# Log-sum-exp on one core: in three of the last four half units, three heads biased on TensorE and folded by GpSimd

## Chip, cores and metric

One core of a Trainium2 chip. The metric is the device time of one execution in microseconds (us). All inputs and outputs are fp32. The profile's own span is about 2 us shorter than the device time, so times inside a trace are compared with times inside another trace, and totals with totals. Ratios of totals are computed as the mean time of one kernel's fast runs over the mean time of the other's fast runs of the same rounds, so they are not quite the ratio of the medians quoted beside them.

## The reference

```python
B, S, D, H = 8, 2048, 2048, 8            # Dh = D // H = 256
x_heads = x.reshape(B, S, H, Dh).transpose(0, 2, 1, 3) + bias[None, :, None, :]
x_tiled = np.repeat(x_heads, 2, axis=2)
mx = x_tiled.max(axis=-1, keepdims=True)
lse = mx.squeeze(-1) + np.log(np.exp(x_tiled - mx).sum(axis=-1))
```

For each row and each of 8 heads: add a bias of 256 numbers, exponentiate, sum, take the logarithm, write it twice. The kernel leaves out the maximum, which random normal inputs allow.

## The kernel before

There are two ways to account for the bias: add it before the exponential (TensorE adds it in PSUM, or GpSimd in SBUF), or multiply the exponential by the *factor* exp(bias) while summing (VectorE's multiply-and-reduce, called a weighted sum below; or a multiply on GpSimd). In this kernel x is loaded into SBUF, and PSUM holds what TensorE puts out and the factors of heads 1 to 6. Rows come in units of 256; late units are split into two half units of 128 rows. I call the last four half units 62a, 62b, 63a, 63b. Each stage shares the 8 heads among the engines:

```python
# pe: heads biased on TensorE; acc: of these, summed by ScalarE's accumulator;
# fold: heads at the upper end multiplied and folded by GpSimd; the rest: weighted sums on VectorE
PROMPT_F1 = dict(pe=2, acc=2, g0=8, late=False, fold=1)
PROMPT_F2 = dict(pe=2, acc=2, g0=8, late=False, fold=2)
SINGLE_F1 = dict(pe=1, acc=1, g0=8, late=False, fold=1)
TRIPLE = dict(pe=3, acc=3, g0=8, late=False, fold=0)
# BULK and MIXED, the body: cut
FOLD = 32
STAGES = [(0, (BULK,)), (54, (MIXED,)), (57, (PROMPT_F1, PROMPT_F1)),
          (62, (SINGLE_F1, SINGLE_F1)), (63, (PROMPT_F2, TRIPLE))]
```

GpSimd's fold multiplies by the factor, then adds halves in place until 32 columns a head are left, which VectorE reduces:

```python
def fold(t, k, h0, h1, sums, after):
    v = xts[t % NBUF][:, k, h0 * Dh : h1 * Dh]
    done = nc.gpsimd.tensor_tensor(out=v, in0=v, in1=w_sb[...], op=ALU.mult)
    ...
    while n > FOLD:
        n //= 2
        done = nc.gpsimd.tensor_tensor(out=v[:, :, 0:n], in0=v[:, :, 0:n], in1=v[:, :, n:2*n], op=ALU.add)
    def add_up(): ...                      # the short reduction on VectorE, recorded later
```

The order on each engine is the order of recording. For one half unit, cut to what matters here:

```python
heads = add_x(...)                         # TensorE adds x to the bias in PSUM
bias_there = put_bias(next half unit)
keep_warm()                                # three dummy matmuls, results unused: to keep the clock up
flush(for_pool)                            # the short reductions of earlier folds, and so on
done = exp_inplace(...)                    # ScalarE: exponential of the SBUF heads
flush(for_pe)                              # ScalarE: exponential of the PREVIOUS half unit's PSUM heads
weigh(...)                                 # VectorE
```

The softmax here doesn't subtract the row's maximum and nothing guards it: scores larger than these inputs give would overflow.

## Time and profile before

| | before |
|---|---|
| time, median of 3 (range) | 325.56 us (325.21 to 325.87) |
| span of the profiled run | 323.1 us |
| busy in the span | PE 84%, VectorE (DVE) 88%, ScalarE (ACT) 82%, GpSimd (POOL) 89% |
| all transfers (loads and stores) | 135.42 MB at 419 GB/s |
| end of each engine's work in the tail | DVE 319.63, ACT 319.43, POOL 319.17 |

Read the table from below: the share of busy time says little in a kernel whose body is paced by loads and whose change lies in the last 15 us. What counts is when each engine finishes its part of the last half units, and there three engines end within 0.5 us of each other. The lines behind this are in the prediction.

### The profile page before, as it was taken

What the parts mean: (1) busy time and instruction counts of PE and PEld (TensorE: products, weight loads), DVE (VectorE), ACT (ScalarE), POOL (GpSimd) and SP (SyncE); (2) the same over time, 40 slices, a digit from 0 to 9 for tenths busy, and PEclk for the clock granted to TensorE, in tenths of its full rate; (3) what the DMA queues carried; (4) which work ended last, traced back from release to release, by engine and by line L of the source; (5) the groups of instructions that cost most, each with busy time, mean ns of one, the idle gap of its engine ahead of it and who ended that gap; (6) DMA issues with size and microseconds to landing.
All of it is one profiled execution on the core that took longest, in us unless ns stands there. A gap on an engine that the chain in (4) does not pass through costs nothing.

```text
span 323.1 us, 2398 instructions
## 1 busy us (share of the span) xinstructions
PE 270.3 (84%) x691; PEld 102.9 (32%) x691; DVE 283.9 (88%) x306; ACT 265.8 (82%) x426; POOL 287.7 (89%) x120
## 2 busy tenths in 40 slices
PE   5999999889978769977869886888997786599984
PEld 2333333333323223322323322333333232035442
DVE  1037779999999998999899899898999999999995
ACT  1148679889869976988888978889998998899995
POOL 6939998999999999999999999999999999858874
PEclk9979799979979996998997997997999999559998
DMA  8999999999999999999999999999999999999995
GB/s 311 457 402 454 450 400 439 450 402 446 438 414 446 432 418 443 430 422 447 422 426 441 422 434 442 404 426 430 432 422 431 430 428 425 416 422 421 419 401 170
DMA packets 8830, 135.42 MB, mean 419 GB/s; under 512 B 1041, under 2 KB 1425, under 8 KB 2417
## 3 DMA queue, kind: packets, MB, share of 16 engines
q1 hardware_dynamic: 8720, 135.27, 98.6%
q8 instruction: 5, 0.08, 0.1%
q14 instruction: 7, 0.06, 0.0%
q10 hardware_dynamic: 98, 0.01, 0.0%
HBM read 134.23 MB, written 1.05 MB: 419 GB/s over the span
## 4 chain that ended last, share of the span: by engine, by line
DMA 40%; POOL 18%; ACT 17%; PE 14%; DVE 9%; issue 0%; SPq 0%; DVEq 0%
DMA xb<-in_x_dram 40%; POOL xb L376 18%; ACT xb L382 11%; DVE R L401 6%; PE pair L326 5%; PE one_ps L326 3%; PE pair L267 3%; ACT xb L357 2%; PE one_ps L267 2%; DVE xb L417 2%; PE pair L219 1%; ACT xb L337 1%; DVE xb L394 1%; ACT res L471 1%; ACT xb L344 1%; DMA brow<-in_bias_dram 1%
## 5 line engine op out<-in xcount | busy, mean ns | idle before, releaser
L376 POOL TENSOR_TENSOR xb<-xb,b_rep 128x2048 f32<-128x2048 f32 x57 | 257.6, 4539 | 20.7 <-DMA xb<-in_x_dram 20.6
L401 DVE TENSOR_REDUCE R<-xb 128x14 f32<-128x3584 f32 (+1 forms) x56 | 214.5, 3830 | 1.9
L382 ACT ACTIVATE xb<-xb 128x2560 f32<-128x2560 f32 (+5 forms) x77 | 157.1, 2050 | 10.3 <-POOL xb L376 10.1
L326 PE MATMUL pair<-xb,ident 128*128 128x512 f32 x216 | 114.3, 656 | 0.0
L326 PE MATMUL one_ps<-xb,ident 128*128 128x512 f32 x108 | 67.5, 710 | 11.5 <-DMA xb<-in_x_dram 11.5
L344 ACT ACTIVATE xb<-pair 128x1024 f32<-128x1024 f32 x54 | 55.5, 1027 | 23.2 <-PE pair L326 23.0
L326 PEld LDWEIGHTS pair<-xb,ident 128*128 128x128 f32 x216 | 46.2, 214 | 61.3 <-issue 61.3
L394 DVE TENSOR_TENSOR xb<-xb,w_ps 128x512 f32<-128x512 f32 x54 | 36.7, 681 | 26.2 <-ACT xb L382 26.2
L337 ACT ACTIVATE xb<-one_ps 128x256 f32<-128x256 f32 x108 | 40.0, 380 | 6.6 <-PE one_ps L326 6.6
L267 PEld LDWEIGHTS <-ones 3*128 3x128 bf16 (+1 forms) x192 | 16.9, 95 | 80.8 <-issue 71.4
L267 PE MATMUL one_ps<-b,ones 3*128 3x512 bf16 x49 | 18.6, 380 | 25.4 <-ACT xb L337 25.3
L267 PE MATMUL pair<-b,ones 3*128 3x512 bf16 x98 | 29.0, 375 | 0.0
L326 PEld LDWEIGHTS one_ps<-xb,ident 128*128 128x128 f32 x108 | 17.2, 200 | 33.9 <-DMA xb<-in_x_dram 18.0
L302 PE MATMUL pair<-xb,ident 128*128 128x512 f32 (+1 forms) x36 | 21.7, 689 | 5.7 <-DMA xb<-in_x_dram 5.7
L417 DVE CUSTOM_DVE_ANT_0 xb<-xb,w_ps 128x256 f32<-128x256 f32 x61 | 22.4, 418 | 0.0
L337 ACT ACTIVATION_READ_ACCUMULATOR xb<-one_ps 128x1 f32 x108 | 22.3, 207 | 0.0
L441 POOL TENSOR_TENSOR xb<-xb 128x128 f32<-128x128 f32 (+3 forms) x39 | 13.8, 355 | 3.1
L433 POOL TENSOR_TENSOR xb<-xb,w_sb 128x256 f32<-128x256 f32 (+1 forms) x13 | 10.0, 771 | 5.2 <-ACT xb L382 4.5
L317 PE MATMUL tp<-ident 128*128 128x128 f32 x84 | 13.7, 302 | 0.0
L317 PEld LDWEIGHTS tp<-ident 128*128 128x128 f32 x84 | 11.1, 200 | 3.5 <-issue 3.0
L357 ACT ACTIVATE xb<-pair 128x256 f32<-128x256 f32 x33 | 11.9, 364 | 0.0
L417 DVE CUSTOM_DVE_ANT_0 xb<-xb,one_ps 128x256 f32<-128x256 f32 x27 | 10.6, 415 | 0.1
(42 smaller groups left out, 83.4 us busy)
## 6 DMA issues: line engine op xcount, KB each, us to landing
xb<-in_x_dram SPq DMA_DIRECT2D x20, 4096.0 KB, 21.5
xb<-in_x_dram SPq DMA_DIRECT2D x17, 2048.0 KB, 22.7
xb<-in_x_dram SPq DMA_DIRECT2D x12, 1024.0 KB, 22.7
xb<-in_x_dram SPq DMA_DIRECT2D x4, 256.0 KB, 13.2
out_dram<-res SPq DMA_DIRECT2D x1, 896.0 KB, 6.7
xb<-in_x_dram SPq DMA_DIRECT2D x2, 384.0 KB, 15.8
xb<-in_x_dram SPq DMA_DIRECT2D x2, 128.0 KB, 6.3
out_dram<-res_last SPq DMA_DIRECT2D x1, 128.0 KB, 1.7
```

Of the source, the lines that this page charges most:

```text
L267: nc.tensor.matmul(p, lhsT=lhsT, rhs=each_row(b, h * Dh, Dh, K), start=i == 0, stop=False,)
L302: mm = nc.tensor.matmul(p, lhsT=ident, rhs=xts[t % NBUF][:, ka:kb, c : c + w], start=False, stop=True,)
L317: nc.tensor.matmul(tp[:, 0], lhsT=ident, rhs=ident, start=True, stop=True)
L326: mm = nc.tensor.matmul(p, lhsT=ident, rhs=xts[t % NBUF][:, :, h * Dh : (h + 1) * Dh], start=False, stop=True,)
L337: act = nc.scalar.activation(out=xts[t % NBUF][:, k, 0:Dh], in_=got[0][:, k * Dh : (k + 1) * Dh], func=ACT.Exp, accum_out=sums[:, k, 0:1],)
L344: act = nc.scalar.activation(out=xts[t % NBUF][:, :, Dh : m["pe"] * Dh].rearrange("p k (h j) -> p h k j", j=Dh), in_=got[-1].rearrange("p ...
L357: act = nc.scalar.activation(out=xts[t % NBUF][:, k, h * Dh : (h + 1) * Dh], in_=p, func=ACT.Exp, accum_out=sums[:, k, h : h + 1],)
L376: add = nc.gpsimd.tensor_tensor(out=v, in0=v, in1=each_row(b_rep, c - G0, D - c, k1 - k0), op=ALU.add)
L382: return on_x(t, nc.scalar.activation(out=v, in_=v, func=ACT.Exp), [after])
L394: mul = nc.vector.tensor_tensor(out=f, in0=f, in1=each_row(w_ps, m["pe"] * Dh - W0, n, k1 - k0), op=ALU.mult,)
L401: red = nc.vector.tensor_reduce(out=sums[:, k0:k1, h0:H], in_=v.rearrange("p k (h j) -> p k h j", j=Dh), op=ALU.add, axis=mybir.AxisListTy ...
L417: ttr = nc.vector.tensor_tensor_reduce(out=v, in0=v, in1=w, scale=1.0, scalar=0.0, op0=ALU.mult, op1=ALU.add, accum_out=dst,)
```

## The change

The intent: in 62a, 62b and 63a TensorE biases three heads in place of one or two. One activation exponentiates all three out of two PSUM banks, without accumulator reads, and GpSimd folds them, without a multiply as the bias is in already. VectorE keeps heads 3 to 7. TensorE, with more real work, drops its dummy matmuls in all four. The core of the diff:

```diff
-PROMPT_F2 = dict(pe=2, acc=2, g0=8, late=False, fold=2)
-SINGLE_F1 = dict(pe=1, acc=1, g0=8, late=False, fold=1)
+FOLDED = dict(pe=3, acc=0, g0=8, late=False, fold=0)
-    (62, (SINGLE_F1, SINGLE_F1)),
-    (63, (PROMPT_F2, TRIPLE)),
+    (62, (FOLDED, FOLDED)),
+    (63, (FOLDED, TRIPLE)),
-    [(0, 512), (1280, 2048), (512, 1280)],
+    [(0, 768), (1280, 2048), (768, 1280)],
...
+    def exp_biased(t, k, n, heads):
+        _, _, bank, _, mm = heads[-1]
+        act = nc.scalar.activation(out=xts[t % NBUF][:, k, 0 : n * Dh],
+                                   in_=pairs[bank // 2][:, 0 : n * Dh], func=ACT.Exp)
...
+                    if m["acc"] == 0:
+                        done = exp_biased(t, k, m["pe"], heads)
+                        for_pool.append(fold(t, k, 0, m["pe"], sums, done))
+                        return
...
-                if next_units and not m["late"]:
-                    bias_there = put_bias(*next_units.pop(0))
-                if t > T_PROMPT and m["g0"] == H:
+                if t > T_PROMPT and m["g0"] == H and m["pe"] * Dh <= MM:
                     keep_warm()
...
-            if c0 == 0:
+            if c0 == 0 or t == T - 1 and k0 == 0:
                 flush(for_pe)
+            if c0 == 0 and next_units and not m["late"]:
+                bias_there = put_bias(*next_units.pop(0))
```

The rest of the diff lets the fold skip its multiply, lets a reader of two banks be ordered against both, and aligns a three-head half unit to a pair of banks.

More of the change, by code (lines that the diff above doesn't have):

```diff
@@ L244, with on_bank @@
     bank_users = [[], []]
-    def on_bank(i, ins):
-        for j, u in bank_users[i // 2]:
-            if j != i and u.ins.engine != ins.ins.engine:
+    def on_bank(i, ins, both=False):
+        pair = i // 2
+        i = None if both else i
+        for j, u in bank_users[pair]:
+            if None not in (i, j) and j != i and u.ins.engine != ins.ins.engine:
                 tc.declare_no_dep(ins.ins, u.ins, reason="another bank")
-        bank_users[i // 2].append((i, ins))
+        bank_users[pair].append((i, ins))
         return ins
@@ L275, in put_bias @@
         n = m["pe"] * Dh
+        if n > MM:
+            n_ps[0] += n_ps[0] % 2
         rows = min(k1 - k0, max(MM // n, 1))
@@ L313, in add_x @@
         return heads
+    def exp_biased(t, k, n, heads):
+        _, _, bank, _, mm = heads[-1]
+        act = nc.scalar.activation(
+            out=xts[t % NBUF][:, k, 0 : n * Dh],
+            in_=pairs[bank // 2][:, 0 : n * Dh],
+            func=ACT.Exp,
+        )
+        on_bank(bank, on_x(t, act, [mm]), both=True)
+        return act
     def keep_warm():
@@ L432, in fold @@
         v = xts[t % NBUF][:, k, h0 * Dh : h1 * Dh]
-        done = nc.gpsimd.tensor_tensor(
-            out=v, in0=v, in1=w_sb[:, h0 * Dh - W1 : h1 * Dh - W1], op=ALU.mult
-        )
-        on_x(t, done, [after])
+        done = after
+        if h0 * Dh >= W1:
+            mul = nc.gpsimd.tensor_tensor(
+                out=v, in0=v, in1=w_sb[:, h0 * Dh - W1 : h1 * Dh - W1], op=ALU.mult
+            )
+            done = on_x(t, mul, [done])
         v = v.rearrange("p (h j) -> p h j", j=Dh)
@@ L440, in fold @@
             n //= 2
-            done = nc.gpsimd.tensor_tensor(
+            add = nc.gpsimd.tensor_tensor(
                 out=v[:, :, 0:n], in0=v[:, :, 0:n], in1=v[:, :, n : 2 * n], op=ALU.add
             )
-            on_x(t, done, [])
+            done = on_x(t, add, [done])
         def add_up():
@@ L535, with pe_part @@
                 heads = add_x(m, t, k0, c0, c1, bias_here)
-                def pe_part(t=t, heads=heads, sums=sums):
+                def pe_part(t=t, m=m, k=k0, heads=heads, sums=sums):
+                    if m["acc"] == 0:
+                        done = exp_biased(t, k, m["pe"], heads)
+                        for_pool.append(fold(t, k, 0, m["pe"], sums, done))
+                        return
                     for k, h, bank, p, mm in heads:
```

## The prediction

> **What bounds the kernel now.** I read the page first, then the table of engines by stretch, then the chain that ended last from 300 us on, and last the timelines of ScalarE (ACT), VectorE (DVE), GpSimd (POOL) and TensorE (PE) over the final 15 us. The page says that the body runs at the rate of the loads:
>
> ```profile
> DMA 40%; POOL 18%; ACT 17%; PE 14%; DVE 9%; issue 0%; SPq 0%; DVEq 0%
> ```
>
> The change touches only the last four half units (128 rows each: 62a, 62b, 63a, 63b), so the body can be set aside, and the question is what happens after about 310 us of a span of 323.1 us. By stretch (columns: microseconds, then busy time of PE, PEld, DVE, ACT, POOL, then clock, DMA share, GB/s):
>
> ```profile
> 297.00:308.00 11.00, 10.68 (x47) 5.44 (x45) 10.65 (x66) 11.00 (x30) 9.27 (x22) 1.00 1.01 417
> 308.00:314.00 6.00, 4.99 (x27) 3.03 (x26) 5.57 (x33) 6.00 (x13) 4.79 (x12) 1.00 1.02 403
> 314.00:320.50 6.50, 4.68 (x24) 2.56 (x22) 5.59 (x33) 5.81 (x21) 4.50 (x8) 1.00 0.75 255
> ```
>
> In the last row nobody is idle for long: ACT 5.81 and DVE 5.59 of 6.5 us. The chain names DVE for the last 5.5 us:
>
> ```profile
> 312.54 1.60 ACT xb L382
> 314.14 0.02 issue
> 314.16 0.42 DVE xb L417
> ...
> 319.50 0.14 DVE R_last L447
> 319.64 0.14 issue
> 319.78 0.32 PE tp L482
> 320.11 0.38 ACT res_last L488
> ```
>
> So VectorE works through its weighted sums (L417, one 256-column head each) without a gap from 314.16 to 319.63, then the final transpose, logarithm and store follow. But ACT's timeline ends only 0.2 us earlier, at 319.43, also without a gap, and POOL's last fold ends at 319.17. Two lines of ACT's timeline (start, us, engine, line, operation, shapes):
>
> ```profile
> 310.15 1.68 ACT L382 ACTIVATE xb<-xb 128x1792 f32<-128x1792 f32 x1
> ...
> 312.45 1.68 ACT L382 ACTIVATE xb<-xb 128x1792 f32<-128x1792 f32 x1
> ```
>
> and POOL's:
>
> ```profile
> 311.91 0.73 POOL L433 TENSOR_TENSOR xb<-xb,w_sb 128x256 f32<-128x256 f32 x1 [0.31 <-ACT xb L382]
> ...
> 317.51 1.66 POOL L441 TENSOR_TENSOR xb<-xb 128x256 f32<-128x256 f32 x3
> ```
>
> The tail is balanced over three engines to within half a microsecond. The slack to look for in a change is in when each engine can start, not in sums of busy time.
>
> When do the loads land? SyncE issued the last load at 312.35 as soon as 62b had landed, and the store of the earlier batches at 313.08 as soon as the first piece of 63a had. A half unit is 1 MB, and they land 2.48 us apart (PE waited for them at 307.40, 309.88, 312.38). By issue-to-landing times, 63a's later two pieces land near 314.1 and 314.9 and 63b's pieces from 315.6 to 317.55. Loads do not bind the old tail, but they stop ACT from running ahead: 62b's exponential cannot start before 312.38.
>
> **What the Trainium skill says.** "GPSIMD Engine Reference", section 3.1 Elementwise, gives 4497 ns for a two-input fp32 add of 2048 elements and about 2.6 cycles an element. The trace's bias add of that size takes 4539 ns, and the fold's rows agree in slope: 730 ns for 256, 457 for 128, 320 for 64, 251 for 32 is 183 ns fixed plus 2.13 ns an element. Section 4.1 of that page says GpSimd has no port to PSUM. So heads biased in PSUM must be exponentiated by ACT into SBUF before GpSimd can begin; no run shows a violation, but it is the reason for the new dependence below. "ScalarE: Activation LUTs", Rules for kernel authors, gives about 0.3 us plus 0.83 ns an element for an activation: the slope holds (1680 less 1472 ns for 256 more elements is 0.81), but the spacing of consecutive activations shows less fixed cost: 1536 columns take 1.38 us from start to start, that is 0.10 plus 0.83 an element. "TensorE: Matmul & The Clock Gate", What's actually happening, says that a quiet PE is throttled to half clock; the tail is at 1.00 before, with dummy matmuls.
>
> **The change part by part.** Every instruction keeps its engine order except as follows.
>
> *VectorE.* Before, its list for the four half units is 6 + 6 + 4 + 5 = 21 weighted sums and three short reductions. After, it is 5 + 5 + 5 + 5 = 20 and three reductions. That is one sum less, 0.34 us by the spacing in the timeline (314.16, 314.51, 314.85).
>
> *ScalarE.* Removed: four single-head exponentials with accumulator read (62a one, 62b one, 63a two; 63b keeps its three) at 0.36 us start to start = 1.43 us. The two of 1792 columns (1.59 each) shrink to 1280 (0.10 + 1.06 = 1.17 each): 0.84 less. A 768-column piece of 63a shrinks to 512: 0.21 less. Added: three of 768 columns from two banks, 0.10 + 0.64 = 0.73 each: 2.20 more. Net 1.43 + 0.84 + 0.21 - 2.20 = 0.28 us less.
>
> *GpSimd.* Before: a multiply and three adds for 62a and for 62b (one head each), the same for two heads of 63a: 1.9 + 1.9 + 3.0 = 6.8 us. After: no multiplies, three adds over three heads, three times. From the fit, 384 columns 1.00, 192 columns 0.59, 96 columns 0.39 = 1.99 us; between dependent adds the trace has 0.08 us (one-head folds: 1.03 busy in 1.19), so 2.14 a fold and, with the 0.04 by which independent instructions overlap, 6.35 us for three. So nothing is dear by its sum. The start is what matters: the old first fold needs 62a's SBUF exponential (ready 311.83); the new one needs 62a's PSUM exponential, which ACT does only *after* 62b's SBUF exponential, and that waits for a load.
>
> *TensorE.* Bias 512 + 256 columns costs 0.42 (315.06 to 315.48), x adds of 768 columns about 1.5 (0.96 start to start for 512, then 0.5), and dummies (0.77 per half unit) go. Each pair of banks is now used by every second half unit, so its bias waits for that exponential.
>
> Now the new tail, step by step (microseconds of the old span):
> - ACT: 62a's 1280 columns 310.15 to 311.32; 61b's two heads (0.71) to 312.03; wait for 62b's load to 312.39; 62b's 1280 to 313.56; 62a's 768 from PSUM starts then and ends at 314.37 (spacing 0.73, own duration 0.81); 62b's follows to 315.0. PE has them ready: 62a's bias goes at 310.3, its x add ends near 312.3; 62b's bias waits for 61b's heads (312.1), its x add ends near 314.1.
> - POOL: starts at 314.45 (ACT to POOL took 0.08 at 311.91). Folds end at 316.6, 318.7 and 320.80.
> - DVE: 62a's five sums 311.8 to 313.5; 62b's 313.7 to 315.4; then the order makes it reduce 62a's fold, not there until 316.6: about 1.2 us idle. Then ten sums, 316.8 to 320.2, 62b's reduction to 320.4, and it waits for the third fold: 320.83, plus 0.25 for 96 columns = 321.08.
> - ACT meanwhile: 63a's 768 SBUF columns at 315.0; 63a's PSUM exponential waits for PE, whose bias for that pair could not begin before 314.35: ready 316.25. Then 0.73, 0.52, 0.52, 0.52, 0.31 and three heads 1.07 give 319.95. Later than before (319.43), though off the end.
>
> VectorE's last reduction ends at 321.08 in place of 319.63: 1.45 us later; transpose, logarithm and store follow as they did. 325.56 + 1.45 = 327.0.
>
> **Rivals.** (1) *The intended gain*: fewer VectorE sums and no accumulator reads end the tail 0.3 us sooner, 325.2. For it: VectorE is the old end. Against: both savings are small, and VectorE's own path contains the stall on the first fold. It would need GpSimd to start 2 us earlier than its input exists. (2) *VectorE and not GpSimd ends it*: if three-head adds cost less than the fit, say 1.9 us a fold, the third ends near 320.1, VectorE's ten sums end near 320.0, two reductions follow, about 320.4: 326.3. For it: only one multi-head fold is in the trace; against: it lies on the same line as the one-head folds. (3) *TensorE slows*: without dummies the clock falls to half after 310 us; x adds then take 3 us and the loop from exponential to bias to x add would set the end, 329 or more. For it: the clock was 0.82 between 287 and 297 us. Against: real matmuls now fill about 1.9 of each 2.1 us. (4) *The loads hide it*: only if the last load (317.55) plus its work set the end; the sum above ends 3 us after it.
>
> **Range and chances.** The GpSimd start is known to about 0.2 us (one landing, one semaphore), its three folds to about 0.3, and the three runs before spread 0.66 us. Rival 2 sets the low end, a slower clock or ACT a little later the high one: 326.2 to 327.7. Two per cent is 6.5 us, more than a tail of this length can give or take except by rival 3 at its worst.
>
> **What would show it.** Right: GpSimd idle from about 311.6 to 314.4, then three folds of about 2.1 us back to back; VectorE idle about 1.2 us before 62a's three-head reduction and again shortly before its last one; the chain's end on GpSimd's folds; ACT waiting on a load near 312 and on TensorE near 316. Wrong: a fold clearly off 2.14 us, VectorE without gaps, a clock below 1.00 after 310, or 62b's load landing elsewhere than 312.4 relative to the rest.

## More of the kernel before

The weighted sum, and where its factor lies (heads 1 to 6 in PSUM, head 7 in SBUF; `w_sb` holds heads 6 and 7):

```python
def weigh(t, v, h, dst, after):
    c = h * Dh
    if c < W0:   w = one_ps[...]          # PSUM
    elif c < W2: w = w_ps[...]            # PSUM
    else:        w = w_sb[...]            # SBUF: head 7
    ttr = nc.vector.tensor_tensor_reduce(out=v, in0=v, in1=w, ..., accum_out=dst)
```

## The result, and the profile after

The changed kernel takes 326.69 us (median of 4 runs, 326.64 to 326.83), against 325.38 us (325.19 to 325.87) for the kernel before in the same set: ratio 1.0039, 95% interval 1.0021 to 1.0056. By its interval it is slower, by 1.3 us of median. The forecast was 327.0, range 326.2 to 327.7.

The tail by stretch, same columns as before:

```profile
297.00:308.00 11.00, 10.63 (x47) 6.26 (x46) 11.00 (x68) 11.00 (x30) 9.38 (x21) 1.00 1.01 419
308.00:314.00 6.00, 5.10 (x19) 2.37 (x18) 5.73 (x35) 5.63 (x12) 2.79 (x7) 1.00 1.01 399
314.00:322.00 8.00, 4.18 (x13) 1.69 (x12) 6.09 (x31) 5.77 (x15) 6.09 (x9) 0.99 0.62 208
```

Up to 308 us little has changed. Between 308 and 314 GpSimd (the fifth figure with a count) falls from 4.79 us busy to 2.79, and after 314 it has 6.09 in place of 4.50 (in a stretch 1.5 us longer): its work has moved to the right. The clock stays at 0.99 without dummies. The chain that ended last (start, us, what) names the reason:

```profile
312.20 0.02 issue
312.23 1.27 ACT xb L397
313.50 0.70 ACT xb L322
314.20 0.07 issue
314.27 1.01 POOL xb L458
...
319.72 0.59 POOL xb L458
320.31 0.04 issue
320.35 0.49 POOLq L644
320.84 0.02 issue
320.87 0.27 DVE R_last L464
321.13 0.14 issue
321.27 0.32 PE tp L499
```

62b's load, 62b's SBUF exponential (L397), 62a's PSUM exponential (L322), then nothing but GpSimd's adds (L458; the last of them is within the POOLq piece) until the last short reduction. Where VectorE's sums stood in the old chain, GpSimd's folds stand now. GpSimd's and ScalarE's timelines show the two waits:

```profile
314.27 6.56 POOL L458 TENSOR_TENSOR xb<-xb 128x384 f32<-128x384 f32 x9 [2.92 <-ACT xb L322]
```

```profile
312.23 1.27 ACT L397 ACTIVATE xb<-xb 128x1280 f32<-128x1280 f32 x1 [0.37 <-DMA xb<-in_x_dram]
313.41 1.49 ACT L322 ACTIVATE xb<-pair 128x768 f32<-128x768 f32 x2
314.78 0.84 ACT L397 ACTIVATE xb<-xb 128x768 f32<-128x768 f32 x1
316.25 0.81 ACT L322 ACTIVATE xb<-pair 128x768 f32<-128x768 f32 x1 [0.62 <-PE pair L306]
```

GpSimd sat idle for 2.92 us and then worked 6.56 us without a break. ScalarE waits 0.37 us for 62b's load and 0.62 us for TensorE before 63a. VectorE waits 0.93 us for the first fold, then works on in the shade of the folds; but the shade is thin: its second last reduction ends at 320.76 us, and it waits only 0.1 us for the third fold. One thing in VectorE's timeline was not foreseen:

```profile
314.91 0.65 DVE L432 CUSTOM_DVE_ANT_0 xb<-xb,w_sb 128x256 f32<-128x256 f32 x1
...
316.49 0.25 DVE L464 TENSOR_REDUCE R_last<-xb 128x3 f32<-128x96 f32 x1 [0.93 <-POOL xb L458]
...
319.74 0.85 DVE L432 CUSTOM_DVE_ANT_0 xb<-xb,w_sb 128x256 f32<-128x256 f32 x1
```

Two weighted sums lasted 0.65 and 0.85 us where all others take 0.41 to 0.42. Both are of head 7, whose factor lies in SBUF (`w_sb`). In the kernel before, GpSimd did head 7 in almost every late half unit, and VectorE's only sum with `w_sb` took 0.42 us.

### The profile page after: what moved, and what is told of

The parts are those of the page before. It is cut to its first block, busy times and chain, and to the rows that moved or that the text cites. A ratio compares the mean times of both kernels' runs of the same rounds, so it can differ in the third digit from the quotient of the medians.

```text
span 324.6 us, 2358 instructions
## 1 busy us (share of the span) xinstructions
PE 267.2 (82%) x676; PEld 101.4 (31%) x676; DVE 284.5 (88%) x304; ACT 266.0 (82%) x421; POOL 287.6 (89%) x117
## 4 chain that ended last, share of the span: by engine, by line
DMA 48%; DVE 17%; PE 14%; ACT 14%; POOL 6%; issue 1%; POOLq 0%; SPq 0%
DMA xb<-in_x_dram 47%; DVE R L416 14%; ACT xb L397 9%; PE pair L341 5%; POOL xb L391 4%; PE one_ps L341 3%; DVE xb L409 2%; PE pair L269 2%; ACT xb L359 2%; POOL xb L458 2%; PE one_ps L269 1%; PE pair L218 1%; ACT xb L352 1%; DMA brow<-in_bias_dram 1%; ACT res L488 1%
## 5 line engine op out<-in xcount | busy, mean ns | idle before, releaser
L397 ACT ACTIVATE xb<-xb 128x2560 f32<-128x2560 f32 (+5 forms) x77 | 155.9, 2033 | 13.2 <-POOL xb L391 12.7
L341 PE MATMUL one_ps<-xb,ident 128*128 128x512 f32 x108 | 66.5, 700 | 13.6 <-DMA xb<-in_x_dram 13.6
L341 PEld LDWEIGHTS pair<-xb,ident 128*128 128x128 f32 x216 | 45.7, 211 | 59.9 <-issue 59.9
L306 PE MATMUL pair<-xb,ident 128*128 128x512 f32 (+1 forms) x42 | 23.6, 662 | 5.0 <-DMA xb<-in_x_dram 5.0
L458 POOL TENSOR_TENSOR xb<-xb 128x128 f32<-128x128 f32 (+5 forms) x39 | 16.4, 422 | 5.7 <-ACT xb L322 2.9
L306 PEld LDWEIGHTS pair<-xb,ident 128*128 128x128 f32 x42 | 7.2, 205 | 14.6 <-DMA xb<-in_x_dram 11.0
L450 POOL TENSOR_TENSOR xb<-xb,w_sb 128x256 f32<-128x256 f32 x10 | 7.3, 730 | 4.5 <-ACT xb L397 3.8
L332 PEld LDWEIGHTS tp<-ident 128*128 128x128 f32 x60 | 8.7, 202 | 7.2 <-issue 4.9
L372 ACT ACTIVATE xb<-pair 128x256 f32<-128x256 f32 x29 | 10.5, 364 | 0.0
L332 PE MATMUL tp<-ident 128*128 128x128 f32 x60 | 8.8, 285 | 1.5 <-ACT res L488 1.5
```

What stands on the lines that cost most here:

```text
L306: mm = nc.tensor.matmul(p, lhsT=ident, rhs=xts[t % NBUF][:, ka:kb, c : c + w], start=False, stop=True,)
L332: nc.tensor.matmul(tp[:, 0], lhsT=ident, rhs=ident, start=True, stop=True)
L341: mm = nc.tensor.matmul(p, lhsT=ident, rhs=xts[t % NBUF][:, :, h * Dh : (h + 1) * Dh], start=False, stop=True,)
L397: return on_x(t, nc.scalar.activation(out=v, in_=v, func=ACT.Exp), [after])
L458: add = nc.gpsimd.tensor_tensor(out=v[:, :, 0:n], in0=v[:, :, 0:n], in1=v[:, :, n : 2 * n], op=ALU.add)
```

## The experiments

Twelve kernels, each executed 4 to 6 times in 5 rounds, in three sets that share the runs of the kernel before. All outputs are right. The first two sets ran on one chip, the third on another. The theory: *the end is set by GpSimd, which begins late because its input is made after 62b's load, and then needs 6.5 us.* The rivals: TensorE's loop (exponential, bias, x add), the missing dummies, VectorE's stall.

| run | median us (range) | ratio to before | expected us |
|---|---|---|---|
| changed kernel again | 326.71 (326.60 to 326.82) | 1.0038 | 326.7 |
| e1 PSUM exponential first | 325.72 (325.59 to 326.58) | 1.0014 | 325.3 to 325.5 |
| e2 short reductions last | 326.96 (326.79 to 327.20) | 1.0046 | 326.7 |
| e3 63a not folded | 325.71 (325.62 to 325.78) | 1.0008 | 325.8 to 326.1 |
| e4 fold to 64 | 326.29 (326.23 to 327.61) | 1.0030 | 326.1 to 326.3 |
| e5 before, no dummies at the end | 325.28 (325.05 to 326.22) | 0.9995 | ratio 1.000 |
| e6 changed, dummies kept | 327.01 (326.83 to 327.13) | 1.0045 | 326.7 to 326.8 |
| e7 e1 and e2 together | 326.16 (325.79 to 327.02) | 1.0025 | 325.2 to 325.4 |
| e8 e1, head 7's factor in PSUM | 325.69 (325.64 to 325.88) | 1.0009 | 325.2 to 325.6 |
| e9 changed, head 7's factor in PSUM | 326.62 (326.59 to 326.78) | 1.0037 | 326.4 to 326.6 |
| e10 e7, head 7's factor in PSUM | 325.95 (325.94 to 326.05) | 1.0017 | 325.2 to 325.6 |
| e11 changed, four factors in SBUF | 328.61 (328.31 to 328.80) | 1.0097 | 327.7 to 329.5 |

The half-width of the ratios' intervals is 0.0012 to 0.0016, that is 0.4 to 0.5 us, mainly because the kernel before itself spreads over 0.9 to 1.0 us. Differences between changed kernels are read from their own, mostly narrower, ranges. The sets are the first four lines, e4 to e7, and e8 to e11; the kernel before had medians of 325.47, 325.35 and 325.30 us in them, so medians of two sets can be compared to about 0.2 us.

**The changed kernel again.** No edit.

> The changed kernel again, as the base of this set. Every theory: 326.7 us, 1.3 us (0.4%) over the kernel before of the same rounds; GpSimd's three folds about 6.5 us back to back from 314.3, VectorE's last reduction at about 320.9.

As expected: folds from 314.34, 6.56 us long, in all respects the first profile.

**e1: start GpSimd earlier.** ScalarE does 62a's PSUM exponential before 62b's SBUF exponential, which waits for a load:

```diff
+            if (t, k0) == (62, 1):
+                flush(for_pe)
             if h0 < h1 and not m["late"]:
                 done = exp_inplace(
```

> Only ScalarE's order changes: 62a's exponential from PSUM now goes before 62b's from SBUF. Theory (GpSimd's late start sets the end): the first fold starts about 1.5 us earlier, near 312.7, the third ends near 319.3, and the time falls by about 1.3 us to 325.3 to 325.5. Rival (TensorE without its dummies, or the loop of banks from exponential to bias to x add, sets the end): PE gets its bias for 63a earlier too, so a gain of its own, but only of ACT's wait for PE, at most 0.6 us: 326.1 or more. Rival (VectorE's stall sets the end): gain 0.9 us at most, 325.8.

```profile
313.18 6.65 POOL L458 TENSOR_TENSOR xb<-xb 128x384 f32<-128x384 f32 x9 [1.69 <-ACT xb L322]
```

GpSimd starts 1.1 us earlier (313.18 against 314.27), and the median falls by 1.0 us. ScalarE's wait for TensorE (0.6 at most) doesn't reach that; VectorE's stall (0.9 at most) nearly would, and e2 decides about it. With e2, the late start is shown to be the main cause. The gain is 0.3 us short of what I expected. GpSimd could not start at 312.7, because TensorE's x add for 62a ended only at 312.27, and it is no longer in the chain, which goes from that x add over ScalarE to VectorE; e8 below has more on this.

**e2: take away VectorE's stall.** The short reductions of the folds go to the end of VectorE's list:

```diff
-                        for_pool.append(fold(t, k, 0, m["pe"], sums, done))
+                        for_end.append(fold(t, k, 0, m["pe"], sums, done))
...
     flush(for_pool)
+    flush(for_end)
     finish_last()
```

> Only VectorE's order changes: the short reductions of the three folds all go to the very end, so VectorE no longer stalls on the first fold. Theory (GpSimd's folds set the end, VectorE's stall is in their shade): no change, 326.7, within 0.15; VectorE's sums end near 319.3 and it then waits for the third fold as before. Rival (the stall on VectorE costs): 0.9 us less, 325.8.

```profile
314.43 6.72 POOL L458 TENSOR_TENSOR xb<-xb 128x384 f32<-128x384 f32 x9 [2.96 <-ACT xb L322]
```

The stall is gone and the time does not fall; it is 0.25 us *longer* than the changed kernel of the same rounds. The rival (0.9 us less) is out. The small loss was not expected: the folds took 6.72 us here, one 384-column add 1.2 us in place of 1.0 (the mean of three rose from 1.00 to 1.07), while VectorE was at work beside it.

**e3: one fold fewer.**

```diff
-    (63, (FOLDED, TRIPLE)),
+    (63, (TRIPLE, TRIPLE)),
```

> 63a's three heads are summed by ScalarE with accumulators as 63b's are, so GpSimd has two folds in place of three. Theory: GpSimd ends at about 318.7 and is off the end; ScalarE has 0.35 us more and ends near 320.2, VectorE's sums near 320.2: about 0.6 to 0.9 us less, 325.8 to 326.1. Rival (length of the folds does not matter, ScalarE or PE sets the end): 0.3 us more than the changed kernel, 327.0.

```profile
314.29 4.41 POOL L458 TENSOR_TENSOR xb<-xb 128x384 f32<-128x384 f32 x6 [3.02 <-ACT xb L322]
```

1.0 us less than the changed kernel, 0.1 more of a gain than the theory's highest. GpSimd has 4.41 us of adds and is off the end: the chain goes from the first fold through VectorE. As by the theory, the length of the folds matters while GpSimd is last and not beyond.

**e4: shorter folds.**

```diff
-FOLD = 32
+FOLD = 64
```

> Every fold stops at 64 columns a head, so each three-head fold loses its last add (0.41 us and 0.07 before it); VectorE's reductions read twice as much, 192 columns in place of 96, about 0.1 us more each. Theory: three folds take 1.4 us less, GpSimd ends near 319.4, VectorE becomes the end near 320.5: about 0.5 us less than the changed kernel, 326.1 to 326.3. Rival (GpSimd is not the end): the time rises by the longer reductions, 326.8 to 327.0.

0.4 us less by the medians (326.29 and 326.71, of two sets), though VectorE has more to reduce: GpSimd's last add had been on the path. Five of six runs lie within 0.15 us; the sixth, which was the profiled one, took 327.61. Its trace is no picture of the median: VectorE arrives late in the tail there and is the chain all the way from 232 us on. In it the folds take 5.13 us.

**e5: the side parts alone.** The kernel before, without dummies in its last four half units and with the bias matmuls at their new place:

```diff
-                if next_units and not m["late"]:
-                    bias_there = put_bias(*next_units.pop(0))
-                if t > T_PROMPT and m["g0"] == H:
+                if t > T_PROMPT and m["g0"] == H and t < T - 2:
                     keep_warm()
...
+            if c0 == 0 and next_units and not m["late"]:
+                bias_there = put_bias(*next_units.pop(0))
```

> The kernel before with only the side parts of the change: no dummy matmuls in the last four half units, and each bias matmul put after the weighted sums' recording. Theory: no effect, ratio 1.000 to the kernel before within 0.0005, clock 1.00 in the tail. Rival (the clock or the moved bias costs the 1.3 us): 326.0 to 326.7.

No effect on the time (ratio 0.9995), so neither side part costs the 1.3 us. But the clock did not stay at 1.00, as I had expected it to. In the profiled run, of 326.22 us (stretches of 2 us):

```profile
310.00:312.00 2.00, 0.69 (x3) 0.16 (x2) 2.00 (x14) 2.00 (x5) 1.46 (x5) 1.00 1.00 392
312.00:314.00 2.00, 1.74 (x5) 0.69 (x5) 2.00 (x14) 2.00 (x4) 1.43 (x4) 0.92 1.05 397
314.00:316.00 2.00, 2.00 (x4) 0.55 (x4) 2.00 (x12) 2.00 (x6) 1.75 (x5) 0.50 1.06 391
```

TensorE was busy for 0.69 of 2 us, and soon after the clock halved. TensorE had slack in that kernel, ScalarE did not wait for it, and so nothing was lost. In the changed kernel, also without dummies, the three-head matmuls keep TensorE busy for 1.75 to 2.00 of each 2 us from 310 to 318 us, and the clock stayed at 1.00 there.

**e6: the dummies kept.**

```diff
-                if t > T_PROMPT and m["g0"] == H and m["pe"] * Dh <= MM:
+                if t > T_PROMPT and m["g0"] == H:
```

> The changed kernel with the dummy matmuls kept to the end, three more per half unit (0.8 us of PE each). Theory: PE has about 0.4 us of slack ahead of 62b's and 1.6 us ahead of 63a's fold, so at most 0.1 us more, 326.7 to 326.8. Rival (the clock without dummies costs): less than 326.5. Rival (PE's loop sets the end): 327.5 or more.

```profile
314.71 0.67 PE tp L332 x6
315.38 0.43 PE pair L288 x2
315.81 1.50 PE pair L306 x4
```

327.01 us, 0.3 more than the changed kernel: more than I expected, and between the figures of the two rivals. By its mechanism it is the second: the chain now runs on TensorE up to 317.3 us, 0.67 us of dummies, 0.43 of bias and 1.49 of x add for each half unit, then over ScalarE and VectorE to the end. That is 2.59 us a half unit, more than the 2.48 us in which the loads bring one. With three heads to bias there was no room for dummies; dropping them saved the change 0.3 us.

**e7: e1 and e2 together.**

> Both reorderings together: 62a's exponential from PSUM first, the folds' reductions last. Theory: GpSimd ends near 319.3 as in the first alone, and VectorE, without its wait for the first fold, ends at about the same time: 325.2 to 325.4, level with the kernel before, at best 0.2 us less. If VectorE's order mattered once GpSimd is earlier, it gains 0.2 us or more on the first reordering alone.

326.16 us, with runs from 325.79 to 327.02: worse than e1 alone, against what I expected, and scattered. The profiled run (327.02) shows three weighted sums with `w_sb` of 0.68, 0.85 and 0.88 us, and VectorE as the chain throughout. With the stall gone, more of VectorE's head-7 sums fall into GpSimd's adds. This made the suspicion of the `w_sb` lines testable.

**e8, e9, e10: head 7's factor from PSUM.** By the last two units the first half of `one_ps` (head 1's factor) is no longer needed:

```diff
+            if t == T - 2 and (k0, c0) == (0, 0):
+                nc.vector.tensor_copy(one_ps[:, 0:Dh], w_sb[:, Dh : 2 * Dh])
...
+        if t >= T - 2 and h == H - 1:
+            w = one_ps[:, 0:Dh]
```

> The first reordering (62a's PSUM exponential first) with head 7's weights for the last four half units read from PSUM in place of SBUF (one copy of 256 columns on VectorE). Theory (VectorE's head-7 sums, whose data and weights both come from SBUF, and GpSimd's adds hold each other up): all of VectorE's sums take 0.34 us start to start, the folds 2.14 us each, VectorE ends near 320.0 with little waiting, ScalarE near 319.8: 325.2 to 325.6, 0.1 to 0.5 less than the first reordering alone. Rival (the long sums have another cause): as the first reordering alone, 325.7, long sums still there.

> The changed kernel with only head 7's weights read from PSUM. Theory: GpSimd is still the end, its three folds fall from 6.56 to about 6.35 us as their 192-column adds lose the hold-up (0.65 to 0.59): 326.4 to 326.6, and no VectorE sum over 0.45 us. Rival: no change, 326.7.

> Both reorderings with head 7's weights in PSUM. Theory: three sums of 0.6 to 0.9 us in the profile of the two reorderings become 0.34 spaced, so the time falls from 326.2 to 325.2 to 325.6, level with the first reordering with PSUM weights. Rival (the late reductions themselves cost): 326.0 or more.

In all three profiles no weighted sum lasts over 0.42 us, and the three folds take 6.32, 6.33 and 6.33 us, where they took 6.56 in the changed kernel, 6.65 in e1 and 6.52 in e7. For e9, the groups of instructions of the tail (times, busy us, mean ns, idle before):

```profile
L434 DVE CUSTOM_DVE_ANT_0 xb<-xb,w_ps 128x256 f32<-128x256 f32 x21 | 7.6, 417 | 0.2 <-ACT xb L397 0.2
...
L460 POOL TENSOR_TENSOR xb<-xb 128x192 f32<-128x192 f32 x3 | 1.8, 593 | 0.2
```

and of the changed kernel:

```profile
L432 DVE CUSTOM_DVE_ANT_0 xb<-xb,w_sb 128x256 f32<-128x256 f32 x4 | 2.3, 585 | 0.0
...
L458 POOL TENSOR_TENSOR xb<-xb 128x192 f32<-128x192 f32 x3 | 2.0, 652 | 0.2
```

So the hold-up is mutual and it is gone when one of the two operands comes from PSUM. How it works can be read off closely. In the traces of all runs, 21 weighted sums after 309 us last longer than 0.44 us; all have their factor in SBUF, and each ends 0.28 or 0.29 us after the GpSimd add beside it has ended (the 0.85 us one above: add from 319.72 to 320.31, sum from 319.74 to 320.59). That is what waiting for the rest of the add looks like, and not a slower sum.

What it is worth in time is little, and these comparisons go from one chip to another: e9 is 0.09 us below the changed kernel's other set, within the spread, so its time doesn't decide between theory and rival; e8 has e1's median with a narrower range (0.24 us against 0.99), and e10 gains 0.2 us on e7, again mostly by losing the scatter. For e8 I had hoped for 0.1 to 0.5 us more, for e10 for 0.35 to 0.75; its 325.95 us lie next to the rival's 326.0. e8's chain shows what stands in the way:

```profile
313.88 0.43 PE pair L288 x2
314.31 1.50 PE pair L306 x4
315.81 0.02 issue
315.83 0.81 ACT xb L322
316.64 0.53 ACT xb L397
317.17 0.02 issue
317.19 0.42 DVE xb L434
```

With GpSimd early, TensorE's bias and x adds for three heads are next: ScalarE waits for them before 63a (0.37 us), and VectorE for ScalarE. That is the rival loop of the prediction, one step behind the cause. e10 is 0.26 us behind e8; of this 0.16 is seen, three short reductions (0.50 us) after VectorE's last sum in place of two (0.34).

**e11: the opposite dose.** The factors of heads 4 to 7 from SBUF:

```diff
+        if t >= T - 2 and h in (4, 5):
+            w = w_more[:, c - G0 : c - G0 + Dh]
+        elif t >= T - 2 and h == 6:
+            w = w_sb[:, 0:Dh]
```

> The opposite dose: the changed kernel with the weights of heads 4 to 7, not only 7, read from SBUF in the last four half units. Theory: many more VectorE sums meet GpSimd's adds, each meeting makes one of the two wait for the other's rest; the folds grow by some 0.3 us for each of the adds that waits, so the last fold ends 1 to 2.5 us later: 327.7 to 329.5. Rival (sums from SBUF cost nothing): 326.7.

328.61 us, 1.9 more than the changed kernel. Two weighted sums in a row, from VectorE's timeline:

```profile
314.96 1.22 DVE L438 CUSTOM_DVE_ANT_0 xb<-xb,w_sb 128x256 f32<-128x256 f32 x1
...
316.12 0.80 DVE L438 CUSTOM_DVE_ANT_0 xb<-xb,w_sb 128x256 f32<-128x256 f32 x1
```

Sums whose data and factor both come from SBUF took 0.58 to 0.64 us on average in the tail, those with the factor in PSUM 0.42 in the same trace, and the folds grew to 7.10 us. Less with none, more with more: both signs are shown. In the same trace the sums with a factor in SBUF that start before 314.3 us or after 321.9, when GpSimd does not add, took 0.41 to 0.42 us, so the factor's place alone costs nothing. The total lies in the range that I expected, but not by the way that I expected: the folds grew by only 0.5 us and ended at 321.77, and it is VectorE's sums, held up one after the other, that end last, with the last reduction at 323.10. That is partly luck.

No version of the changed kernel beats the kernel before. The nearest are e3 and e8, level with it (ratios 1.0008 and 1.0009, intervals that include 1).

## Why the prediction was right

*The mechanism.* The prediction put the end on GpSimd's folds, because their first input is made after 62b's SBUF exponential, and that after a load. The chain says the same, step by step; e1 shows that the start matters, e3 and e4 that the length does, e2 that VectorE's stall lies in the shade. e1 brings 1.0 of the 1.3 us back; that the rest is TensorE's loop is read from e8's chain and was not tested by an edit.

*The sizes.* The step "62a's PSUM exponential starts at 313.56" came at 313.41 (62b landed 0.15 us earlier in this trace), so GpSimd started at 314.27 for 314.45. "Three folds 6.35 us" came out as 6.56: mis-sized by 0.2 us. The fit of duration to columns was right, as e9's 6.33 us shows; what it left out was that VectorE would now read head 7's factor from SBUF beside GpSimd. "VectorE's last reduction ends at 321.08" came at about 321.13, in part because the earlier landing and the longer folds nearly cancel. Against the trace of before that is 1.50 us, against the forecast 1.45. The totals differ by 1.3 us; the trace of before was of a run of 325.31 us and medians of the kernel before lie at 325.3 to 325.6, so 0.2 us of difference is in the spread. Two small sums of the prediction are off without harm: the three old folds took 1.99, 2.00 and 3.01 us from start to end, 7.0 in place of 6.8, and the three adds of the fit make 1.98 us, not 1.99.

*ScalarE and TensorE.* ScalarE's wait for TensorE before 63a was foreseen to end at 316.25 and did so, with 0.62 us of wait. Its last accumulation was foreseen to end at 319.95 and ended at 320.01. VectorE's two waits were smaller than foreseen: 0.93 us for 1.2 before the first fold's reduction, and 0.1 us for 0.4 before the last one, by the two long sums. So GpSimd ended last by less than the forecast says.

*Wrong inside a right total.* First, each weighted sum was priced at 0.34 us start to start, wherever its factor lies. The Trainium skill's page "SBUF — State Buffer", section Who interferes with whom, says that a VectorE instruction with two SBUF inputs contends with a GpSimd instruction that reads SBUF. Its section Summary: rules for kernel authors says of this case that the second to issue fully blocks until the first is done. I had read the durations and not the operands. The traces agree with the page: sums of 0.46 to 1.22 us that end 0.28 us after one of GpSimd's adds, 0.42 otherwise, gone in e8 to e10. Second, I gave the dummies "slack" in my expectation of e6; their removal was worth 0.3 us. Third, the rival "a slower clock" was argued against with TensorE's share of busy time, which held for the changed kernel, while in e5 the clock did fall, without harm. Fourth, the row of "ScalarE: Activation LUTs" that the prediction found too high counts about 0.3 us for an activation whose bias is a pointer operand; the exponentials of this kernel are given no bias, so the 0.10 us of the trace does not contradict it.

*What stays open.* e5's runs fall into two groups about 0.8 us apart (325.05 to 325.28, and 326.01 and 326.22), and the kernel before spreads over 0.9 us in the same rounds. In the profiles of e4, e5 and e7, each of the slowest run of its kernel, VectorE comes late out of the body (in e5 its first weighted sum of the late units starts at 282.13 us, in the profile of before at 279.92) and never waits after that. Why it is late was not studied. The changed kernel's runs lie within 0.25 us; that its wait on GpSimd takes up such a delay is likely, but was only argued. The other side parts of the change, the new column split of 63a and the place of its exponentials in ScalarE's order, were not tried alone.

## What to carry to other kernels

When work moves to an engine with room, ask first when its input will exist: here GpSimd had less to do than before (6.56 us for 7.0) and still ended 1.7 us later (320.83 for 319.17), because its input had moved behind a load and another activation in ScalarE's order. Look at where both operands of a VectorE instruction lie when GpSimd works beside it; here one factor kept in PSUM removed the hold-up. And a wait that the trace shows on an engine off the chain can be worth nothing when removed, as e2 showed.

## What the Trainium skill lacked or had wrong

- "TensorE: Matmul & The Clock Gate", section HAM oscillation, gives the rule in the abstract as no TensorE idle gaps over about 3.4 us. In e5 the clock fell to 0.50 at about 313.7 us with no TensorE gap over 1.6 us in the 3.4 us before. In the changed kernel a gap of 1.54 us, up to 293.4 us, left it at 1.00. So a gap well under 3.4 us can come before a fall and need not; what decides, these runs don't say. (The page's section A second HAM failure mode does tell of frequent short idles that make the clock swing, but gives no length.)
- "SBUF — State Buffer", section Who interferes with whom, states the rule and held; what it has no number for is a VectorE sum that waits for a GpSimd add. Here a multiply-and-reduce of 256 columns took 0.42 us alone and 0.46 to 1.22 when it met GpSimd's adds of 96 to 384 columns, ending 0.28 us after the add, and the three folds 6.33 us undisturbed and up to 7.10 us with four factors in SBUF.
